# The differences of the blocks of w_co: built and split ahead, kept in DRAM, loaded as parts

## The chip, the core and the metric

The kernel runs on one core of a Trainium2 chip. Its time is the device time of one launch in microseconds (us). The core has five engines that run their own instruction streams in order and wait for one another through semaphores: TensorE (PE, matrix products), VectorE (DVE), ScalarE (ACT), GpSimd (POOL) and SyncE (SP), which here does nothing but issue DMA transfers, one after the other.

## The reference, cut to what matters

One layer of an encoder over 1024 tokens of width 1024 in float32: a mixer (window attention beside a gated delta rule), cross attention from the tokens into 256 memory tokens, and a SwiGLU feed-forward network (FFN). Each part is wrapped in RMS norms and added to the residual. The change lies in the second part:

```python
h2 = rms_norm(x1, g_cross_pre)
q = h2 @ w_cq
...
p = softmax(q_h @ k_h.T / 16)
o = concat(p @ v_h)
x2 = x1 + rms_norm(o @ w_co, g_cross_post)
```

## The kernel before, in words

**Precision.** TensorE multiplies in a reduced float32 format (F32R). Each operand is therefore split into a high and a low part by `split` (L100): ACT casts the high part (L103), DVE, or POOL where that is asked for, subtracts it from the source for the low part (L104). A product is three matmuls: high x high, high x low, low x high (`three`). One matmul of 128 x 128 by 128 x 512 is the unit. `load_w` (L119) issues one transfer of 512 KB into a `wraw` tile (L126) and splits it into `whi` and `wlo`; there are two buffers of each. Blocks under `tc.high_priority(AHEAD)` are moved up by the scheduler at build time; apart from that it lays out each engine's order from the program's order and its own estimate.

**Cross attention.** Tokens are worked in two halves of 512, hf 0 and 1. `cross_q(hf)` (L1136) makes the queries in eight products, one for each 128 columns of w_cq: load, split (the low part on POOL), 24 matmuls into `pcq`, eviction and split into `q`. `cross_attention(q, hf)` (L1145) goes over four heads: scores `pcs`, maximum and scaling on DVE (L1159, L1160), exponential on ACT (L1164), reciprocal and normalisation on DVE (L1166, L1167), transposes `pct`, their split into `cph` and `cpl`, and the product with the values `pco` (L1183). The scheduler weaves the second half's query products into the first half's attention. For the second half the evictions also make differences with the first half's result, kept in `oraw` (L1193 to L1202).

**The product with w_co.** `o @ w_co` is done in the seven-product way on 2 x 2 blocks: four blocks of `o` (two token halves by two halves of the width) and four blocks of w_co, b11, b12, b21, b22, each 512 x 512. Seven block products of 48 matmuls replace eight, in exchange for sums and differences of blocks. Two products use w_co as it is: (0, 0) and (1, 0), loaded by `load_w`. Then come, in order: Y with `s3_` by the difference in b12; Y further with `a22` by that in b21; X with `part` by that in b22; X further, tile by tile (`by_tile`), with `s1_` by that in b11, for token rows 4 to 7; X further with `s4_` by w_co's fourth block, for token rows 0 to 3. The four raw blocks are loaded into the two `wco` tiles in eight transfers of 512 KB (L1218) that stand behind the second half's query weights on SP. Differences are made in place by `minus` on DVE (L1275): those of b11 and b12 inside the first product (`sums`), those of b22 and b21 inside the second (`later`). `weight_part` (L1237) splits each 128-row slice of a difference just ahead of its use into two `wpart` buffers of a ring of nine, 16 splits in all.

**Row ends.** As the tiles of the last two products come, `second_rows` and `first_half_rows` finish the token rows: evictions (L1314), squares on ACT (L1279), gains (L1317), then `finish`: the scale (POOL's power, L1287), the residual (L1288), its store, the next norm's squares on ACT (L1291), and the normalised row (L1295 on ACT or L1297 on DVE). Residual rows come by transfers into `xr` tiles or into the `wco` tiles, which are free by then (L1351).

**What follows.** The normalised rows are transposed (`ptn`, L1394), split with the gain (L106, L107) into `x1h`, `x1l` (rows 4 to 7) and into the parts and sums T1 to T4, X22 (rows 0 to 3, L1412 to L1426). Rows 4 to 7 feed the first half of the first FFN products, and all rows the rest (`EARLY`, L1439 to L1462); their gate and up weights are two `load_w` each. After these the FFN goes on by pairs (`pair_weights`, L1478), which the change does not touch.

## Time and profile before

| | us |
|---|---|
| three runs | 1539.69, 1540.47, 1540.54 (median 1540.47) |
| the profiled execution | 1545.09 |
| its span, from the first instruction to the last | 1543.4 |
| cross attention of both halves and products with w_co | about 649 to 873 |
| row ends, transposes and first FFN products | about 867 to 955 |

A line of a view by stretches gives the stretch and its length, then for each engine its busy time in us and in brackets its instructions, then PE's granted clock as a share of full speed, the DMA engines' busy share, and what they moved in GB/s. A group's line gives source line, engine, operation, output<-inputs, shapes and count, then busy us and mean ns, then idle time before and what ended it. A line of waits gives the waiting engine and line, what it waited for, total us, times and the longest. The chain of waits is followed back from the last instruction; each piece has its start, its length and what ran or what was waited for. PE's busy time counts pipelined matmuls, so overlapping ones are not added twice.

### The profile page before, as it was taken

Reading aid. Unit: us, or ns where it says so; the run is one execution under the profiler, and the core shown is the slowest. Engines: PE = TensorE matmul, PEld = TensorE weight load, DVE = VectorE, ACT = ScalarE, POOL = GpSimd, SP = SyncE. Lnnn points to the kernel's source line nnn. Section 1 sums busy time; section 2 is a strip of 40 time slices with the busy share of each in tenths; the row PEclk is TensorE's granted clock in tenths of the full one; section 3 lists DMA queues with packets and bytes.
Section 4 is the critical chain, followed back from the end, with each engine's and each line's share of the span. In section 5 each row is a group of like instructions: output and inputs, shape, how many; then the busy total and the mean of one; then the engine's idle time right before and its main releaser. Section 6 shows DMA issues by size and latency. Waiting matters only on the chain.

```text
span 1543.4 us, 21078 instructions
## 1 busy us (share of the span) xinstructions
PE 1479.7 (96%) x7403; PEld 1240.7 (80%) x7403; DVE 1111.7 (72%) x1794; ACT 743.2 (48%) x1516; POOL 405.1 (26%) x404
## 2 busy tenths in 40 slices
PE   6999999998999899999999888999999999999997
PEld 5888888877889778888887667888888888888786
DVE  6868999786789865536388986776867554696665
ACT  5678821457557664555345664323223332454532
POOL 2020221311336203242100822343443332000021
PEclk9999999999999999999999899999999999999999
DMA  6235575857987674441332434333533333863354
GB/s 204 77 106 149 145 194 151 218 158 200 311 284 223 205 270 156 152 129 56 94 125 96 165 127 139 123 118 121 167 123 100 109 103 103 315 212 98 105 176 165
DMA packets 264167, 241.91 MB, mean 157 GB/s; under 512 B 33769, under 2 KB 203646, under 8 KB 264062
## 3 DMA queue, kind: packets, MB, share of 16 engines
q1 hardware_dynamic: 264061, 240.57, 49.8%
q8 instruction: 58, 0.95, 0.3%
q14 instruction: 48, 0.39, 0.1%
HBM read 171.02 MB, written 66.88 MB: 154 GB/s over the span
## 4 chain that ended last, share of the span: by engine, by line
PE 63%; DVE 10%; DMA 8%; ACT 4%; issue 3%; POOL 2%; SPq 2%; DVEq 0%; POOLq 0%; ACTq 0%
PE pD L1439 8%; PE pE L1439 8%; PE pA L1439 7%; PE pcq L261 6%; PE pdX L1630 6%; PE pmg L1068 5%; PE pdA L1630 4%; PE pB L1439 4%; PE psc L809 3%; PE pst L1254 2%; PE pdD L1630 2%; PE pg L261 1%; PE pco L1183 1%; PE pdX L1727 1%; PE pcs L1157 1%
## 5 line engine op out<-in xcount | busy, mean ns | idle before, releaser
L103 ACT CAST whi<-wraw 128x1024 fp32r<-128x1024 f32 x96 | 100.8, 1051 | 161.1 <-issue 38.2
L104 POOL TENSOR_TENSOR wlo<-wraw,whi 128x1024 fp32r<-128x1024 f32 x38 | 92.9, 2446 | 186.9 <-ACT whi L103 183.9
L261 PE MATMUL pg<-hlo,whi 128*128 128x512 f32 x352 | 139.7, 397 | 0.0
L261 PE MATMUL pg<-hhi,whi 128*128 128x512 f32 x352 | 139.1, 396 | 0.0
L261 PE MATMUL pg<-hhi,wlo 128*128 128x512 f32 x352 | 138.6, 394 | 0.0
L1439 PE MATMUL pA<-b,whi 128*128 128x512 f32 x352 | 113.3, 401 | 1.8 <-ACT m L1456 1.6
L104 DVE TENSOR_TENSOR wlo<-wraw,whi 128x1024 fp32r<-128x1024 f32 x58 | 74.8, 1291 | 44.2 <-ACT whi L103 41.6
L1439 PEld LDWEIGHTS pA<-b,whi 128*128 128x128 f32 x352 | 67.0, 193 | 16.8 <-ACT m L1456 2.7
L1630 PE MATMUL pdX<-dhl,whi 128*128 128x512 f32 x264 | 76.1, 390 | 1.5 <-DVE zv L1689 0.7
L261 PEld LDWEIGHTS pg<-hhi,whi 128*128 128x128 f32 x352 | 66.6, 189 | 13.5 <-ACT hhi L103 0.2
L261 PEld LDWEIGHTS pg<-hhi,wlo 128*128 128x128 f32 x352 | 66.5, 189 | 12.9
L261 PEld LDWEIGHTS pg<-hlo,whi 128*128 128x128 f32 x352 | 66.5, 189 | 12.8
L1517 POOL TENSOR_TENSOR act<-act,up 128x512 f32<-128x512 f32 x33 | 49.8, 1509 | 93.7 <-DVE up L1516 61.8
L1439 PE MATMUL pA<-b,wlo 128*128 128x512 f32 x176 | 69.8, 398 | 1.3 <-DVE wlo L104 1.3
L103 ACT CAST whi<-araw 128x1024 fp32r<-128x1024 f32 (+1 forms) x36 | 35.3, 982 | 68.0 <-PE pdX L1630 27.6
L104 DVE TENSOR_TENSOR wlo<-araw,whi 128x1024 fp32r<-128x1024 f32 (+1 forms) x36 | 40.8, 1133 | 36.0 <-ACT whi L103 35.9
L1489 POOL TENSOR_TENSOR sr<-wraw 128x512 f32<-128x512 f32 x22 | 30.0, 1365 | 130.8 <-DMA wraw<-in_w_gate_up_dram 129.7
L1664 POOL TENSOR_SCALAR frs<-sq 128x1 f32<-128x1 f32 x8 | 12.0, 1498 | 194.3 <-ACT jk L1649 193.4
L286 DVE SCALAR_TENSOR_TENSOR acc<-cp,cols,acc 128x1024 f32<-128x1024 f32 x48 | 62.1, 1296 | 0.1
L1630 PEld LDWEIGHTS pdX<-dhl,whi 128*128 128x128 f32 x264 | 49.3, 188 | 12.7 <-issue 1.1
L1439 PE MATMUL pB<-s,s1h 128*128 128x512 f32 x176 | 54.4, 390 | 3.2 <-ACT s1h L103 3.2
L1490 DVE TENSOR_TENSOR sr<-sr,wraw 128x512 f32<-128x512 f32 x22 | 36.7, 1666 | 26.7 <-POOL sr L1489 26.7
(478 smaller groups left out, 4292.1 us busy)
## 6 DMA issues: line engine op xcount, KB each, us to landing
wraw<-in_w_gate_up_dram SPq DMA_DIRECT2D x52, 512.0 KB, 3.9
kv<-d_kv SPq DMA_DIRECT2D x32, 512.0 KB, 7.2
wraw<-in_w_in_dram SPq DMA_DIRECT2D x22, 512.0 KB, 4.8
b<-in_w_down_dram SPq DMA_DIRECT2D x20, 512.0 KB, 7.7
araw<-d_as SPq DMA_DIRECT2D x20, 512.0 KB, 3.7
pz<-d_pz SPq DMA_DIRECT2D x32, 256.0 KB, 6.9
wraw<-in_w_ckv_dram SPq DMA_DIRECT2D x16, 512.0 KB, 5.7
wraw<-in_w_out_dram SPq DMA_DIRECT2D x16, 512.0 KB, 3.7
```

What stands on the lines that cost most here:

```text
L103: nc.scalar.copy(hi, src)
L104: (eng or nc.vector).tensor_tensor(lo, src, f32(hi), ALU.subtract)
L261: nc.tensor.matmul(p_, w[:, k, :], ah[a][:, k, :], start=(k == 0 and i == 0), stop=(k == nk - 1 and i == 2))
L286: nc.vector.scalar_tensor_tensor(acc, cp[:, t:t + S], taps[t], acc, ALU.mult, ALU.add)
L809: nc.tensor.matmul(out[:, d, h, :], lt[:, d, h, :], rt[:, d, h, :], start=True, stop=True)
L1068: nc.tensor.matmul(pp[t], act[a][:, k, tt], w_[:, kk, :], start=(k == 0 and i == 0), stop=(k == KT - 1 and i == 2))
L1254: nc.tensor.matmul(bank, a[:, tt], w, start=(start and i == 0), stop=(stop and i == 2), skip_group_check=not check)
L1439: nc.tensor.matmul(out_, w[a][:, k, :], xx[b_][:, k, :], start=(start and k == 0 and i == 0), stop=(k == HK - 1 and i == 2), skip_group_ch ...
L1489: nc.gpsimd.tensor_tensor(s[0], b_[:, 0:HK], b_[:, HK:], ALU.add)
L1490: nc.vector.tensor_tensor(s[1], s[0], a_[:, 0:HK], ALU.subtract)
L1517: nc.gpsimd.tensor_tensor(o_, o_, up, ALU.mult)
L1630: nc.tensor.matmul(banks[t], a[:, k - k0, tt], w, start=(first and k == 0 and i == 0), stop=(k == NB - 1 and i == 2), skip_group_check=not ...
```

## The change

The differences are no longer made from resident blocks inside the products. Ahead of the second half's query products the program now states, for each of four 128-row slices k: four loads of 256 KB (the slices of the four raw blocks) into `wpart` buffers, four differences on DVE, four splits, and eight stores of 256 KB of the parts into eight DRAM tiles `d_t` (`sum_out`). The scheduler weaves this into the query products and the first half's attention. When the products come, the parts are loaded: those of the third difference (b12) and second (b22) slice by slice into the ring (`from_ring`, eight transfers of 256 KB each), those of the fourth (b21) and first (b11) whole into tiles of opA (`resident`, four transfers of 512 KB each). The `wco` tiles and the 8 transfers of 512 KB into them are gone, as are `weight_part`, `minus`, `sums` and `later`.

With the space that becomes free: `y7` gets a tile of its own; the difference of the two halves' attention (`s3raw`) is kept in float32, so that the second half's eviction takes one DVE subtraction instead of two; the residual rows 0 to 5 go into tiles of opA (`two_rows`), rows 6 and 7 into `xr`; the first gate and up weights of the FFN are loaded and split by `load_w` at the start of Y (`first_gate`) instead of in the EARLY loop. Instructions of PE, ACT and POOL are the same in number; DVE has four fewer, and SP has 787 transfers to issue instead of 723.

```diff
--- before.py
+++ after.py
@@ -1022,6 +1022,8 @@
     def operand(pool_, tag):
         if tag == "s1":
             return [Halves(opB, b0), Halves(opB3, "b3")]
+        if tag == "s0":
+            return [Halves(opA, f"s0{c}") for c in "hl"]
         if tag in places:
             return [p_.tile([P, KT, HALF], F32R, tag=t, name=t) for p_, t in places[tag]]
         return [pool_.tile([P, KT, HALF], F32R, tag=f"{tag}{i}", name=f"{tag}{i}") for i in range(2)]
@@ -1189,19 +1191,23 @@
                     continue
                 k = ct % HK
                 if ct < HK:
-                    d_ = tx.tile([P, HALF], F32, tag="cs", name="cs")
+                    d_ = s3_raw()[:, k]
                     nc.vector.tensor_tensor(d_, raw[:, k], po, ALU.subtract)
                     split(q[0][:, k], q[1][:, k], d_)
                     continue
                 split(q[0][:, ct, :], q[1][:, ct, :], po)
                 d_ = tx.tile([P, HALF], F32, tag="cs", name="cs")
-                nc.vector.tensor_tensor(d_, po, f32(q[0][:, k]), ALU.subtract)
-                nc.vector.tensor_tensor(d_, d_, f32(q[1][:, k]), ALU.subtract)
+                nc.vector.tensor_tensor(d_, po, s3_raw()[:, k], ALU.subtract)
                 split(*(t[:, k] for t in s2_part()), d_)
                 nc.vector.tensor_tensor(raw[:, k], raw[:, k], d_, ALU.add)
                 nc.vector.tensor_tensor(raw[:, ct], raw[:, ct], d_, ALU.subtract)
 
-    part = []
+    part, kept = [], []
+
+    def s3_raw():
+        if not kept:
+            kept.append(opA.tile([P, HK, HALF], F32, tag="s0h1", name="s3raw"))
+        return kept[0]
 
     def s2_part():
         if not part:
@@ -1210,13 +1216,30 @@
 
     q0 = cross_q(0)
     cross_attention(q0, 0)
+    d_t = {n: [dram.tile([P, HK, HALF], F32, name=f"d_t{n}{c}") for c in "hl"] for n in (1, 2, 3, 4)}
+
+    def wpart(dt):
+        return rg.tile([P, HALF], dt, tag="wpart", name="wpart", bufs=9)
+
+    def sum_out(n, k, src):
+        parts = [wpart(F32R) for _ in range(2)]
+        split(*parts, src)
+        for d_, t in zip(d_t[n], parts):
+            nc.sync.dma_start(d_[:, k], f32(t))
+
+    for k in range(HK):
+        r12, r11, r22, r21 = (wpart(F32) for _ in range(4))
+        for t, i, j in ((r12, 0, 1), (r11, 0, 0), (r22, 1, 1), (r21, 1, 0)):
+            nc.sync.dma_start(t, w_co[(HK * i + k) * P:(HK * i + k + 1) * P, j * HALF:(j + 1) * HALF])
+        nc.vector.tensor_tensor(r11, r12, r11, ALU.subtract)
+        nc.vector.tensor_tensor(r12, r22, r12, ALU.subtract)
+        sum_out(3, k, r12)
+        sum_out(1, k, r11)
+        nc.vector.tensor_tensor(r22, r22, r11, ALU.subtract)
+        nc.vector.tensor_tensor(r21, r21, r22, ALU.subtract)
+        sum_out(2, k, r22)
+        sum_out(4, k, r21)
     q1 = cross_q(1)
-    wco = [opA.tile([P, KT, HALF], F32, tag=f"s0{i}", name="wco") for i in range(2)]
-    (b11, b12), (b21, b22) = ((t[:, 0:HK], t[:, HK:KT]) for t in wco)
-    for b_, i, j in ((b12, 0, 1), (b11, 0, 0), (b22, 1, 1), (b21, 1, 0)):
-        for k0 in (0, 2):
-            nc.sync.dma_start(b_[:, k0:k0 + 2], w_co[(HK * i + k0) * P:(HK * i + k0 + 2) * P, j * HALF:(j + 1) * HALF]
-                              .rearrange("(k p) n -> p k n", p=P))
     cross_attention(q1, 1)
     L2.close()
     Lk.close()
@@ -1234,11 +1257,20 @@
     def blocks(t):
         return t[:, 0:HK], t[:, HK:KT]
 
-    def weight_part(b_, k):
-        with tc.high_priority(AHEAD):
-            dh, dl = (rg.tile([P, HALF], F32R, tag="wpart", name="wpart", bufs=9) for _ in range(2))
-            split(dh, dl, b_[:, k])
-        return dh, dl
+    def from_ring(n):
+        parts = []
+        for k in range(HK):
+            parts.append([wpart(F32R) for _ in range(2)])
+            for t, d_ in zip(parts[k], d_t[n]):
+                nc.sync.dma_start(f32(t), d_[:, k])
+        return parts
+
+    def resident(n, tags):
+        hl = [opA.tile([P, HK, HALF], F32R, tag=t_, name="tw") for t_ in tags]
+        for k0 in (0, 2):
+            for t, d_ in zip(hl, d_t[n]):
+                nc.sync.dma_start(f32(t[:, k0:k0 + 2]), d_[:, k0:k0 + 2])
+        return [[t[:, k] for t in hl] for k in range(HK)]
 
     def act_part(a, k0):
         if isinstance(a, tuple):
@@ -1253,7 +1285,7 @@
         for i, (a, w) in enumerate(((ah, dh), (ah, dl), (al, dh))):
             nc.tensor.matmul(bank, a[:, tt], w, start=(start and i == 0), stop=(stop and i == 2), skip_group_check=not check)
 
-    def block_product(banks, a, b_, first=True, last=True, extra=None):
+    def block_product(banks, a, b_, first=True, last=True):
 
         for k in range(HK):
             if k % 2 == 0:
@@ -1264,15 +1296,10 @@
                     wh, wl = load_w(w_co[rows:rows + 2 * P, c0:c0 + HALF], 2, HALF)
                 dh, dl = wh[:, k % 2], wl[:, k % 2]
             else:
-                dh, dl = weight_part(b_, k)
+                dh, dl = b_[k]
             for t in range(4):
                 three(banks[t], ah[:, k % 2], al[:, k % 2], dh, dl, slice(t * P, (t + 1) * P), first and k == 0,
                       last and k == HK - 1, first and last)
-            if extra:
-                extra(k)
-
-    def minus(o_, a, b_):
-        nc.vector.tensor_tensor(o_, a, b_, ALU.subtract)
 
     def square_of(src, ch, r):
         jk = tz.tile([P, HALF], F32, tag="junk", name="junk")
@@ -1302,14 +1329,6 @@
     def four(spec):
         return [p_.tile([P, HALF], F32, tag=t_, name="pst") for p_, t_ in spec]
 
-    def sums(k):
-        minus(b11[:, k], b12[:, k], b11[:, k])
-        minus(b12[:, k], b22[:, k], b12[:, k])
-
-    def later(k):
-        minus(b22[:, k], b22[:, k], b11[:, k])
-        minus(b21[:, k], b21[:, k], b22[:, k])
-
     def add(o_, a, b_):
         nc.vector.tensor_tensor(o_, a, b_, ALU.add)
 
@@ -1318,26 +1337,27 @@
 
     LO, HI = slice(0, HALF), slice(HALF, D)
     A = four([PG] * 4)
-    block_product(A, a11, (0, 0), last=False, extra=sums)
+    block_product(A, a11, (0, 0), last=False)
     e_ = opB.tile([P, HK, HALF], F32, tag=b0 + "0", name="p1")
     for t in range(4):
         nc.scalar.copy(e_[:, t], A[t])
-    block_product(A, a12, (1, 0), first=False, extra=later)
+    block_product(A, a12, (1, 0), first=False)
     c11 = opB3.tile([P, HK, HALF], F32, tag="b30", name="c11")
     for t in range(4):
         nc.scalar.copy(c11[:, t], A[t])
+    first_gate = [load_w(w_gate_up[:, c0:c0 + P], KT, P) for c0 in (0, FF)]
     Y = four([PG] * 4)
-    block_product(Y, s3_, b12, last=False)
-    y7 = b12
+    block_product(Y, s3_, from_ring(3), last=False)
+    y7 = opA.tile([P, HK, HALF], F32, tag="s0h0", name="y7")
     for t in range(4):
         add(y7[:, t], e_[:, t], Y[t])
-    block_product(Y, a22, b21, first=False)
+    block_product(Y, a22, resident(4, ("s0l0", "s0l1")), first=False)
     for t in range(4):
         square_of(c11[:, t], 0, t)
         gained(zz[:, t, LO], c11[:, t], LO)
         add(zv[:, t], e_[:, t], Y[t])
     X = four([PN] * 2 + [PX] * 2)
-    block_product(X, tuple(part), b22, last=False)
+    block_product(X, tuple(part), from_ring(2), last=False)
     for t in range(4):
         add(zv[:, t], zv[:, t], X[t])
         square_of(zv[:, t], 0, 4 + t)
@@ -1352,8 +1372,15 @@
         res[r] = place.rearrange("p h n -> p (h n)")
 
     res = {}
-    for r, place in ((4, b21[:, 0:2]), (5, b21[:, 2:4]), (6, b22[:, 0:2]), (7, b22[:, 2:4])):
-        residual_row(r, place)
+
+    def two_rows(r, tag):
+        t = opA.tile([P, HK, HALF], F32, tag=tag, name="xr2")
+        for i in range(2):
+            residual_row(r + i, t[:, 2 * i:2 * i + 2])
+
+    two_rows(4, "s0l1")
+    residual_row(6)
+    residual_row(7)
 
     def by_tile(a, w, last, then):
         for t in range(4):
@@ -1374,9 +1401,9 @@
         add(zz[:, t, HI], e_[:, t], X[t])
         row_end(zz[:, t], t)
 
-    by_tile([act_part(s1_, k) for k in (0, 2)], [weight_part(b11, k) for k in range(HK)], False, second_rows)
-    for r, place in ((0, None), (1, None), (2, b11[:, 0:2]), (3, b11[:, 2:4])):
-        residual_row(r, place)
+    by_tile([act_part(s1_, k) for k in (0, 2)], resident(1, ("s0h1", "s0l0")), False, second_rows)
+    two_rows(0, "s0h1")
+    two_rows(2, "s0h0")
     with tc.high_priority(AHEAD):
         for k in (0, 2):
             wr = wp.tile([P, 2, HALF], F32, tag="wraw", name="wraw")
@@ -1448,7 +1475,7 @@
         sg = te.tile([P, 512], F32, tag="sg", name="sg0")
         w, A = [], []
         for i, c0 in enumerate((f * P, FF + f * P)):
-            whi, wlo = load_w(w_gate_up[:, c0:c0 + P], KT, P)
+            whi, wlo = first_gate[i] if e == 0 else load_w(w_gate_up[:, c0:c0 + P], KT, P)
             w.append(((whi[:, 0:HK], wlo[:, 0:HK]), (whi[:, HK:], wlo[:, HK:])))
             A.append(pg.tile([P, 512], F32, tag="pg", name="pA0"))
             product(A[i], w[i][0], X11)
```

## Prediction, made before the changed kernel ran

> **What bounds the kernel now.** I read the page's first part first, then a table of busy time by stretch, then what the TensorE (PE) waits for, then single instructions.
>
> ```profile
> span 1543.4 us, 21078 instructions
> PE 1479.7 (96%) x7403; PEld 1240.7 (80%) x7403; DVE 1111.7 (72%) x1794; ACT 743.2 (48%) x1516; POOL 405.1 (26%) x404
> ...
> 690.00:745.00 55.00, 55.00 (x294) 47.20 (x293) 28.34 (x49) 25.70 (x60) 15.07 (x7) 1.00 0.23 68
> 745.00:776.00 31.00, 31.00 (x153) 25.99 (x152) 11.97 (x20) 11.81 (x24) 4.20 (x2) 1.00 0.41 136
> 776.00:857.00 81.00, 77.81 (x387) 64.34 (x387) 71.13 (x117) 45.53 (x94) 9.23 (x4) 1.00 0.30 104
> 857.00:873.00 16.00, 16.00 (x72) 13.25 (x71) 13.72 (x20) 8.17 (x17) 13.54 (x13) 1.00 0.51 166
> 873.00:897.00 24.00, 15.48 (x64) 10.85 (x62) 19.68 (x26) 16.77 (x31) 21.26 (x24) 0.79 0.33 131
> 897.00:960.00 63.00, 57.42 (x251) 45.46 (x252) 47.40 (x65) 34.46 (x55) 9.24 (x7) 0.97 0.47 144
> ```
>
> After the stretch and its length stand PE, weight loads, VectorE (DVE), ScalarE (ACT) and GpSimd (POOL) in busy us, then PE's granted clock, the DMA share and GB/s. PE is the bound nearly everywhere: 96% of the span. From 690 to 776 (the second half's query products and both halves' cross attention) it is never idle, while DVE works about half of the time. From 776 to 857, where DVE makes the weight differences and their splits, DVE is at 71.13 of 81 and PE loses 3.2 us. Between the last w_co product and the first FFN products (873 to 897) PE stands for 8.5 us of 24 and its clock falls. So the change can win only in 776 to 908, and can lose only in 690 to 776 or through late data.
>
> ```profile
> PE pB L1439 <- ACT s1h L103: 3.2, 2, 2.0
> PE ptn L1394 <- DVE b L107: 2.5, 2, 2.0
> ...
> PE ptn L1394 <- DVE zl L1297: 1.6, 1, 1.6
> PE pco L1183 <- DVE cpl L104: 1.5, 2, 0.9
> ...
> PE pst L1254 <- DVE zl L1314: 1.2, 1, 1.2
> ...
> PE pst L1254 <- DVE wlo L104: 0.5, 1, 0.5
> ```
>
> These are PE's waits from 690 to 960 (total us, times, longest). The pco and pst rows, 1.5 + 1.2 + 0.5 = 3.2 us, are the whole idle time of the third stretch.
>
> **What the change takes out of 776 to 873.**
>
> ```profile
> L104 DVE TENSOR_TENSOR wpart<-wco,wpart 128x512 fp32r<-128x512 f32 x16 | 11.4, 715 | 1.4 <-PE pst L1254 1.4
> L1275 DVE TENSOR_TENSOR wco<-wco 128x512 f32<-128x512 f32 x16 | 10.3, 685 | 3.2 <-DMA wco<-in_w_co_dram 3.2
> ...
> L1199 DVE TENSOR_TENSOR cs<-cs,b 128x512 f32<-128x512 f32 x4 | 2.6, 684 | 0.0
> ...
> L103 ACT CAST wpart<-wco x16: 602/621/650, 778.3 to 848.7; 128x512 fp32r<-128x512 f32 x16
> ```
>
> 16 differences (10.3 us) and 16 low parts (11.4) leave DVE, 16 casts of 0.62 (9.9 us) leave ACT; four more DVE subtractions (2.6) are gone for good, since the difference of the two score halves is kept raw. DVE goes from 71.1 + 13.7 = 84.8 to 84.8 - 24.3 = 60.5 us of 97. The differences now come ready from DRAM, so the attention's cpl, the eviction zl and wlo no longer queue behind them. I take all 3.2 us of PE's waits as gone; the bounds are 0 (they only change their releaser) and 3.2.
>
> **The tail.** What DVE still owed at the last product's end sets the idle time after it.
>
> ```profile
> 856.41 4.66 DMA wraw<-in_w_gate_up_dram
> ...
> 867.27 1.21 DVE wco L1288
> ...
> 946.28 4.59 DMA wraw<-in_w_gate_up_dram
> ...
> 862.37 11.05 PE L1254 MATMUL pst<-part,b 128*128 128x512 f32 x48
> ...
> 883.19 1.12 PE L1394 MATMUL ptn<-ident,zl 128*128 128x128 f32 x4 [2.02 <-DVE b L107]
> ...
> 892.53 0.33 PE L1394 MATMUL ptn<-ident,zz 128*128 128x128 f32 x1 [0.66 <-DVE zz L1297]
> ...
> 893.85 0.44 PE L1394 MATMUL ptn<-ident,zz 128*128 128x128 f32 x2 [0.52 <-DVE b L107]
> 896.03 0.44 PE L1394 MATMUL ptn<-ident,zz 128*128 128x128 f32 x2 [1.74 <-ACT zz L1295]
> 897.08 0.74 PE L1439 MATMUL pA<-b,whi 128*128 128x512 f32 x2 [0.61 <-ACT m L1456]
> ...
> 907.15 0.50 PE L1439 MATMUL pA<-b,wlo 128*128 128x512 f32 x1 [1.26 <-DVE wlo L104]
> ```
>
> The first three lines are of the chain of waits, the others of PE's instructions, with the idle time before one in brackets. The first row end (L1288, row 4) starts at 867.27. Its tile was finished after the first 12 of 48 matmuls of the by-tile product before 862.37; at 11.05 / 48 = 0.23 us each that is 862.37 - 36 x 0.23 = 854.1. It came 13 us late, because ACT and DVE had stood for the FFN's gate weights (4.66 us) and DVE had a backlog. In the new order those weights are asked for at the start of Y, two products earlier, and DVE's backlog is shorter; with an eviction, a gain and a square of about 0.65 us each, partly overlapped, and POOL's power row 4 can end near 860, some 7.5 us earlier, and rows 4 to 7 are normalised near the product's end. The first pair of FFN products needs all four of those rows, eight transposed tiles and their evictions, so PE resumes at the product's end + 8.8, by my count of DVE's new order, where it was 883.19 - (862.37 + 11.05) = 9.8: 1.0 us won (bounds 0 and 3). Rows 0 to 3, which hold up the second part, do not wait behind rows 4 to 7 any more; I put them ready at + 18 instead of + 25. The idle times there, 0.66 + 0.52 + 1.74 + 0.61 + 1.26 = 4.8 us, are taken as gone (bounds 0 and 4.8).
>
> ```profile
> 876.00:880.00 4.00, 2.89 (x13) 2.25 (x13) 3.93 (x7) 3.28 (x7) 2.71 (x5) 0.65 0.02 8
> 880.00:884.00 4.00, 1.98 (x7) 1.26 (x7) 4.00 (x8) 3.71 (x7) 3.20 (x4) 0.50 0.65 262
> 884.00:888.00 4.00, 4.00 (x15) 3.23 (x14) 4.00 (x4) 2.88 (x4) 3.84 (x5) 0.57 0.17 67
> ...
> 896.00:900.00 4.00, 3.36 (x10) 2.56 (x11) 2.42 (x2) 1.52 (x3) 2.71 (x4) 0.71 0.36 132
> 900.00:904.00 4.00, 4.00 (x17) 3.14 (x17) 1.91 (x3) 1.78 (x3) 0.34 (x1) 0.87 0.01 4
> ```
>
> After each group of idle times PE works at a lower granted clock. The first drop (2.89 x 0.35 + 1.98 x 0.5 + 4.00 x 0.43 = 3.7 us) stays, as most of its idle time stays. The second (3.36 x 0.29 + 4.00 x 0.13 = 1.5 us) goes with the 4.8.
>
> **What it adds to 690 to 776.** The same 32 DVE operations and 16 casts, four rounds of: four loads of 256 KB, four differences, four splits, eight stores of 256 KB. In the built order the rounds lie between DVE positions 825 and 898, the first ahead of the first score maximum (its scaling ran at 693.78, below), the last some 70 operations on: about 690 to 745. DVE goes there from 28.34 to 28.34 + 21.7 = 50.0 us of 55; ACT from 25.7 to 35.6. PE is fully busy there, so nothing can be won; the question is what DVE's lag costs.
>
> ```profile
> 693.78 2.08 DVE L1160 TENSOR_SCALAR cmx<-cmx 128x2 f32<-128x2 f32 x1
> ...
> 693.43 2.40 POOL L104 TENSOR_TENSOR wlo<-wraw,whi 128x1024 fp32r<-128x1024 f32 x1 [4.19 <-ACT whi L103]
> ```
>
> A DVE operation on two columns takes 2.08 us, and ends with POOL's subtraction (695.83). There are seven of these in the stretch, 15.07 us of POOL. If each holds a DVE operation that reads and writes SBUF only (all 32 new ones do) for half its time, that is 7 x 1.2 = 8.4 us, of which the 28.34 already hold some 3: DVE then has about 55 of 55, and lags the attention by up to some 6 us toward the end. PE's order was built with more products left for after the attention (194 matmuls of w_co after its last tile, 160 before: 34 x 0.23 = 7.8 us), so fewer products lie between the attention's steps to cover the lag; against that, from 745 to 776 DVE has 19 us free to catch up. Bounds: 0 and 8 us (the lag uncovered, and 2 more in the first round). I take 3, nearer the low end, as PE shows no wait at all there with DVE half idle, and query products still stand between the attention's steps.
>
> The Trainium skill ("SBUF — State Buffer", section "SBUF: two separate sides") calls the port pair of DVE and GpSimd an exclusive lock held for a whole instruction, which also stops a DVE operation with two SBUF inputs. The two rows agree for the short operation, and by the rule any of the new ones can be held up to 2.4 us; that is the second rival below, priced there from rows.
>
> ```profile
> wraw<-in_w_cq_dram SPq DMA_DIRECT2D x16, 512.0 KB, 4.3
> d_a<-act SPq DMA_DIRECT2D x29, 256.0 KB, 2.8
> ...
> wco<-in_w_co_dram SPq DMA_DIRECT2D x8, 512.0 KB, 7.1
> ...
> 740.47 0.37 SPq L126 DMA_DIRECT2D wraw<-in_w_cq_dram  x1
> ...
> 751.74 1.05 ACT L103 CAST whi<-wraw 128x1024 fp32r<-128x1024 f32 x1 [3.75 <-issue]
> ```
>
> Transfers: 8 loads of 512 KB (4 MB) become 16 + 24 loads and 32 stores (20 MB), 64 more issues on the one in-order queue of SP. At 0.37 us each that is 24 us of issuing, in a stretch where the queue mostly waits; 12 MB of it in some 55 us, on top of 68 GB/s, is below 300 GB/s. The eight query weights are interleaved with the rounds on SP. The last was issued at 740.47, is landed 4.3 later, and is used at 751.74: 7 us of slack. A round takes a load (4.3, as the larger w_cq load), eight DVE operations (8 x 0.69 = 5.5), the first cast (0.6) and a store (2.8), 13.2 us, some 15 behind the attention's operations, so four end about 750: the last query weight is a few us late inside its slack, cost 0. The reloads are asked for one product or more ahead (a product of 48 matmuls lasts 11 us, a load 2.8 to 7.1): cost 0, bounds 0 and 3, for the parts of the fifth product, whose tiles come free last.
>
> **Sum.** 3.2 + 1.0 + 4.8 + 1.5 = 10.5 won, 3 lost: 7.5 us. The profiled execution took 1545.1 us (span 1543.4 and 1.7 around it), 4.6 above the median of 1540.5, so it gives 1545.1 - 7.5 = 1537.6, and taken off the median 1533.0. With the lag at 0 to 5.5 and the tail's second part half won to wholly won the forecast's own range is 1529 to 1537.4. What this kernel's measurement can tell from no change is 0.2%, 3.1 us: 1537.4 to 1543.6 is the same.
>
> **Rivals.**
> (1) The tail is not won. For: the second part's evictions and T parts follow on a DVE that is 75% busy from 897 to 960, and a wait of 3.2 us for s1h stands at the end of that stretch, behind 4.59 us for gate weights, so time won at 892 can be lost there. Against: those weights are asked for as soon as a buffer is free, so earlier too. Then 3.2 + 1.0 - 3 = 1.2 us: 1539.3.
> (2) DVE saturates: held by POOL, each of the seven subtractions costs it 2 us, 14 in all, and PE's stalls reach their bound of 8. For: the stretched operation above. Against: 31 us of half-idle DVE follow. 10.5 - 8 = 2.5 us: 1538.0 (1535 to 1541).
> (3) Slower: the rounds run through a ring of nine buffers with twelve uses a round, so the next round's loads wait on SP for DVE and for stores to land, and the query weights wait behind them; PE then stands for its weight. The price is four times what a round takes over 15 us, less the 7 us of slack and the 3 by which the last issue may slip. A round of 20 gives 20 - 10 = 10 us and cancels the gain; one of 21.5 gives 26 - 10 = 16, and 1540.5 - 10.5 + 16 = 1546. For: every operation of a round queues behind in-order attention work on DVE and ACT, and a cast that waits for a buffer stops ACT's softmax behind it. Against: DMA at a share of 0.23, and the stores' 2.8 us.
>
> **How the numbers follow.** Forecast 0.48; the same with no lag at all (1527 to 1529) 0.06; rival (1) 0.06; rival (2) 0.12, a third of it still under 1537.4; rival (3) 0.28 over 1543.6 to 1555, as its chain is the longest and least covered by rows. Faster 0.48 + 0.06 + 0.04 = 0.58, same 0.06 + 0.08 = 0.14, slower 0.28. The range 1527 to 1549 leaves out about 0.12, the longer part of rival (3).
>
> **What would show it.** Right: PE 55 of 55 or at least 52 in the stretch of the rounds with DVE above 45; no pst or pco wait over 1 us in the products; the first L1288 within 7 us of its tile; ACT's 4.66 us wait for gate weights gone; one group of idle times after the last product, not two, the clock below 1 only once. Wrong: PE waiting for cpr, cpl or a query cast in the rounds (rival 2), for whi of a query weight, with SP's loads late (rival 3), for a reloaded part; or the second group of idle times standing further on (rival 1).

## The result, and the profile after

The changed kernel ran 14 times beside 14 runs of the kernel before: median 1534.12 us (1530.37 to 1545.67) against 1542.90 (1537.62 to 1549.76); ratio 0.9947, 95% interval 0.9928 to 0.9967. A later set of 11 runs beside 33 gave 0.9968 (0.9957 to 0.9980). By these ratios it is faster by some 5 to 8 us.

These are the first part of the page after, and the same stretches as in the prediction:

```profile
span 1536.2 us, 21190 instructions
PE 1477.0 (96%) x7403; PEld 1241.1 (81%) x7403; DVE 1109.5 (72%) x1790; ACT 742.3 (48%) x1516; POOL 396.3 (26%) x404
...
690.00:745.00 55.00, 52.33 (x276) 43.40 (x275) 44.72 (x79) 32.24 (x74) 14.07 (x6) 1.00 0.78 258
745.00:776.00 31.00, 31.00 (x152) 26.00 (x151) 12.61 (x21) 13.43 (x26) 5.34 (x3) 1.00 0.72 246
776.00:857.00 81.00, 81.00 (x407) 68.68 (x406) 56.76 (x87) 39.02 (x83) 12.60 (x9) 1.00 0.36 121
857.00:873.00 16.00, 14.88 (x69) 11.99 (x67) 13.38 (x23) 10.29 (x20) 9.49 (x14) 1.00 0.80 294
873.00:897.00 24.00, 19.42 (x84) 15.39 (x85) 15.76 (x21) 16.90 (x27) 17.37 (x18) 0.79 0.24 93
897.00:960.00 63.00, 56.18 (x250) 44.99 (x250) 47.84 (x68) 32.01 (x52) 10.85 (x7) 0.97 0.44 137
```

The products from 776 to 857 run without a gap (77.81 of 81 before); DVE is at 56.76 there instead of 71.13. The price stands in the first stretch: 55 - 52.33 = 2.67 us of idle PE where there was none, with the DMA share up from 0.23 to 0.78. Behind the products (857 to 897) PE stands 5.7 us of 40, 8.5 before; but the last stretch lost more than before, 6.8 us instead of 5.6. PE's last product and its instructions that waited after it show where:

```profile
859.74 11.04 PE L1286 MATMUL pst<-part,b 128*128 128x512 f32 x48
...
872.50 0.44 PE L1421 MATMUL ptn<-ident,zl 128*128 128x128 f32 x2 [1.06 <-DVE zl L1324]
...
874.89 0.66 PE L1421 MATMUL ptn<-ident,zl 128*128 128x128 f32 x4 [1.14 <-DVE zz L1333]
878.10 1.22 PE L1466 MATMUL pA<-b,whi 128*128 128x512 f32 x2 [2.56 <-ACT b L106]
880.11 1.12 PE L1421 MATMUL ptn<-ident,zl 128*128 128x128 f32 x4 [0.79 <-DVE b L107]
932.41 0.73 PE L1466 MATMUL pA<-b,whi 128*128 128x512 f32 x2 [3.35 <-ACT m L1483]
938.76 0.73 PE L1466 MATMUL pB<-s0h,s1h 128*128 128x512 f32 x2 [2.03 <-ACT s1h L103]
```

From 880 to 929 nothing waits: the second group of idle times (892 to 907 before) is gone. A new one of 3.35 us stands at 932, at the last of the first FFN products.

To compare kernels without what happens ahead of the change, I count from the first query matmul. The rows of the tiles give it (after the colon min, median and max ns of one, then first and last start); here for after:

```profile
L261 PE MATMUL pcq<-b,whi x128: 386/390/481, 646.8 to 695.6; 128*128 128x512 f32 x128
...
L1286 PE MATMUL pst<-part,b x48: 388/389/393, 859.7 to 870.4; 128*128 128x512 f32 x48
...
L1466 PE MATMUL pB<-s0h,s1h x176: 388/390/500, 938.8 to 1294.1; 128*128 128x512 f32 x176
```

The products end 870.4 - 646.8 = 223.6 us after it (start of the last matmul), the first matmul of the pairs (the pair stage) follows 938.8 - 870.4 = 68.4 later (the tail), and the execution ends at 1536.2 - 646.8 = 889.4. The table has the same for all profiles, and the ratios of the runs.

| kernel | first query matmul at | products end | tail | end | ratio to before (95%) |
|---|---|---|---|---|---|
| before | 648.8 | 224.2 | 72.6 | 894.6 | |
| before again | 643.6 | 223.9 | 74.1 | 896.7 | 1.0012 (0.9998 to 1.0026) |
| after | 646.8 | 223.6 | 68.4 | 889.4 | 0.9947 (0.9928 to 0.9967) |
| after again | 644.7 | 223.7 | 67.8 | 889.7 | 0.9968 (0.9957 to 0.9980) |
| raw slices ahead | 647.7 | 223.4 | 66.1 | 887.2 | 0.9963 (0.9947 to 0.9979) |
| gate weights late | 645.9 | 224.0 | 65.6 | 887.8 | 0.9945 (0.9930 to 0.9959) |
| before, gate weights early | 646.7 | 226.1 | 65.7 | 889.9 | 0.9959 (0.9942 to 0.9975) |
| 24 operations back (place held) | 643.1 | 243.6 | 73.9 | 916.3 | 1.0104 (1.0081 to 1.0126) |
| 24 operations back | 644.7 | 231.8 | 68.3 | 898.3 | 1.0005 (0.9992 to 1.0017) |
| low parts on POOL | 645.6 | 224.3 | 68.7 | 890.6 | 0.9966 (0.9951 to 0.9980) |
| before, gate early, POOL | 643.6 | 227.5 | 66.0 | 891.4 | 0.9957 (0.9941 to 0.9974) |
| ahead and POOL | 645.1 | 221.7 | 69.3 | 888.5 | 0.9967 (0.9954 to 0.9980) |
| ahead, gate late | 642.4 | 219.5 | 68.6 | 886.7 | 0.9955 (0.9939 to 0.9971) |
| differences on POOL | 645.7 | 227.6 | 65.3 | 891.6 | 0.9981 (0.9970 to 0.9991) |

The change's own worth in the traces is 6.1 us: (894.6 + 896.7) / 2 against (889.4 + 889.7) / 2. Of that 0.4 lies in the products and 5.3 in the tail; the rest lies behind the tail. The tail's gain is only in part idle time: PE stands 12.9 and 11.9 us in the tails before, 11.1 and 10.3 after, 1.8 less, while its busy time for the same 258 instructions falls from 59.6 and 62.1 to 57.2 and 57.4, 3.5 less. Another 2.0 us of the difference of the first two spans lies ahead of the first query matmul, which came between 642.4 and 648.8 in 14 profiles: that is spread, and no part of the change. The runs cannot tell kernels apart that differ by 2 or 3 us. The traces from a common point come closer, but two profiles of one kernel still differ there by 2.1 us (before) and 0.3 us (after) at the end.

### The profile page after: what moved, and what is told of

The parts are those of the page before. It is cut to its first block, busy times and chain, and to the rows that moved or that the text cites. A ratio compares the mean times of both kernels' runs of the same rounds, so it can differ in the third digit from the quotient of the medians.

```text
span 1536.2 us, 21190 instructions
## 1 busy us (share of the span) xinstructions
PE 1477.0 (96%) x7403; PEld 1241.1 (81%) x7403; DVE 1109.5 (72%) x1790; ACT 742.3 (48%) x1516; POOL 396.3 (26%) x404
## 4 chain that ended last, share of the span: by engine, by line
PE 70%; DVE 11%; DMA 8%; ACT 6%; issue 3%; SPq 1%; POOL 1%; DVEq 0%; POOLq 0%; ACTq 0%
PE pE L1466 8%; PE pD L1466 8%; PE pA L1466 7%; PE pg L261 6%; PE pmg L1070 6%; PE pdX L1657 6%; PE pcq L261 4%; PE pdA L1657 4%; PE pB L1466 4%; PE pst L1286 3%; PE psc L809 2%; PE pdX L1754 2%; PE pdD L1657 2%; DVE acc L286 2%; DMA wraw<-in_w_ckv_dram 1%
## 5 line engine op out<-in xcount | busy, mean ns | idle before, releaser
L261 PEld LDWEIGHTS pg<-hhi,whi 128*128 128x128 f32 x352 | 66.5, 189 | 13.3 <-ACT hhi L103 0.2
L261 PEld LDWEIGHTS pg<-hhi,wlo 128*128 128x128 f32 x352 | 66.5, 189 | 12.8
L261 PEld LDWEIGHTS pg<-hlo,whi 128*128 128x128 f32 x352 | 66.4, 189 | 12.7
L286 DVE SCALAR_TENSOR_TENSOR acc<-cp,cols,acc 128x1024 f32<-128x1024 f32 x48 | 62.1, 1295 | 0.1
L1691 POOL TENSOR_SCALAR frs<-sq 128x1 f32<-128x1 f32 x8 | 11.9, 1496 | 193.6 <-ACT jk L1676 192.7
L1466 PE MATMUL pB<-s0h,s1h 128*128 128x512 f32 x176 | 54.4, 391 | 3.4 <-ACT s1h L103 3.4
L103 ACT CAST dhl<-b 128x512 fp32r<-128x512 f32 x66 | 40.3, 620 | 31.6 <-PE pdA L1657 13.7
```

The source lines that it names most:

```text
L103: nc.scalar.copy(hi, src)
L261: nc.tensor.matmul(p_, w[:, k, :], ah[a][:, k, :], start=(k == 0 and i == 0), stop=(k == nk - 1 and i == 2))
L286: nc.vector.scalar_tensor_tensor(acc, cp[:, t:t + S], taps[t], acc, ALU.mult, ALU.add)
L1466: nc.tensor.matmul(out_, w[a][:, k, :], xx[b_][:, k, :], start=(start and k == 0 and i == 0), stop=(k == HK - 1 and i == 2), skip_group_ch ...
```

## The experiments

**The loss in the rounds.** What ended DVE's waits in the rounds (680 to 745 of after), and pieces of its chain of waits:

```profile
DVE wpart L1234 <- DMA wpart<-in_w_co_dram: 8.9, 4, 3.9
...
DVE wpart L1235 <- DMA wpart<-in_w_co_dram: 1.2, 1, 1.2
...
712.86 5.12 DMA wpart<-in_w_co_dram
718.00 0.70 DVE wpart L1234
```

DVE isn't full there (44.72 of 55). It stands, in order, at the first difference of a round until that round's raw slice has landed, and the attention's maximum, scaling and evictions behind it stand too. SP's queue shows when the raw loads of each round go out:

```profile
685.08 1.95 SPq L1233 DMA_DIRECT2D wpart<-in_w_co_dram  x4
...
698.85 2.90 SPq L1233 DMA_DIRECT2D wpart<-in_w_co_dram  x4
...
712.21 2.26 SPq L1233 DMA_DIRECT2D wpart<-in_w_co_dram  x4
...
727.62 0.38 SPq L1233 DMA_DIRECT2D wpart<-in_w_co_dram  x1
```

They go when the ring has places again, in rounds of 13.8, 13.4 and 15.4 us. To test that this is what costs, the raw slices of three rounds went to a place that is empty until the attention writes it:

```diff
+    def raw_loads(k):
+        ts = [raw[:, HK * (k > 0) + i] for i in range(4)] if k < 3 else [wpart(F32) for _ in range(4)]
...
+    ahead = [raw_loads(0), raw_loads(1)]
     for k in range(HK):
-        r12, r11, r22, r21 = (wpart(F32) for _ in range(4))
+        r12, r11, r22, r21 = ahead[k]
...
+        if 0 < k < 3:
+            ahead.append(raw_loads(k + 1))
+    cross_attention(q0, 0)
```

> The raw slices of the first three rounds land in the still empty tile of the attention's result (oraw) instead of the ring, two rounds at once and ahead of the attention; only the fourth uses the ring. Theory: in the rounds DVE stands in order behind a difference whose raw load is late (7.5 + 1.2 us of waits on it in the profile of after), and this makes PE's 2.7 us of stalls there. Then DVE's waits for raw loads fall under 3 us, PE's stalls between 690 and 745 under 1 us, and the time from the first query matmul to the end of the last w_co matmul falls from 224.0 to 222 or 222.5; about 1.5 us faster than the changed kernel. Rival (DVE is full, held by POOL): the same DVE work is there, so PE's stalls stay at 2 to 3 us and 224.0 stays.

DVE's waits for raw loads fell from 10.1 (8.9 + 1.2) to 3.5 us (2.2 + 1.3). PE's three stalls became one of 2.12, and behind that one stands the fourth round, the only one that still uses the ring:

```profile
719.41 2.03 DVE L1238 TENSOR_TENSOR wpart<-wpart 128x512 f32<-128x512 f32 x1 [2.15 <-DMA wpart<-in_w_co_dram]
721.37 0.68 DVE L104 TENSOR_TENSOR b<-pco,b 128x512 fp32r<-128x512 f32 x1
...
722.10 0.85 PE L1175 MATMUL pct<-ident,cpr 128*128 128x128 f32 x4 [2.12 <-DVE b L104]
```

The difference L1238 waits 2.15 us for its load, takes 2.03 instead of 0.69 (a subtraction of POOL runs from 718.53 to 720.89), and PE waits for the eviction behind it. So the rows show the mechanism at the one stall that is left, but the numbers that were to follow did not come: DVE's waits 3.5 us (under 3 expected), PE's stalls 2.12 (under 1; the rival said 2 to 3), the end of the products 223.4 (222 to 222.5), where a lowered clock took back some 1.4 us. With the gate weights late as well, the order that the build laid out had no such stall:

```diff
     (raw slices ahead, and)
-    first_gate = [load_w(w_gate_up[:, c0:c0 + P], KT, P) for c0 in (0, FF)]
...
-            whi, wlo = first_gate[i] if e == 0 else load_w(w_gate_up[:, c0:c0 + P], KT, P)
+            whi, wlo = load_w(w_gate_up[:, c0:c0 + P], KT, P)
```

> The raw slices ahead together with the gate weights asked for late again: the two single edits had 289.5 and 289.6 us from the first query matmul to the first pair matmul, the changed kernel 292.0. Theory (each took a different loss of the changed kernel away): 287 to 288.5, and some 3 us faster than the changed kernel. Rival (both figures are the changed kernel's own spread): 289 to 292.

```profile
690.00:745.00 55.00, 55.00 (x297) 47.26 (x296) 38.49 (x69) 31.63 (x73) 14.55 (x6) 1.00 0.80 263
```

PE is busy all through the rounds, the products end at 219.5, 4.1 us earlier than in after, with the same DMA traffic (share 0.80) and the same DVE work. So neither the traffic nor the amount of DVE work costs by itself. Of the 4.1 us 2.7 are the stalls; the other 1.4 are PE's busy time for the same 1105 instructions, 219.6 us instead of 221.0, and no run shows why. DVE's and PE's order in the rounds also differs a little from that of the run with the raw slices ahead alone, so the last stall's end is not the loads' alone. But the tail is 68.6 again, so the end comes 2.9 us earlier in the trace, and the runs (0.9955) cannot tell it from the changed kernel. The 288.1 us to the first pair matmul are the theory's (287 to 288.5), the 3 us in the runs can't be seen. Then the rival of a full DVE held by POOL was put to the test by giving POOL the differences:

```diff
-        nc.vector.tensor_tensor(r11, r12, r11, ALU.subtract)
+        nc.gpsimd.tensor_tensor(r11, r12, r11, ALU.subtract)
     (and the other three)
```

> The changed kernel with the 16 differences made by POOL, so that a difference that stands for its raw load no longer stands in DVE's order. Theory (the loss in the rounds is DVE standing in order for raw loads): DVE's waits for them, 8.7 us, vanish, and PE's 2.7 us of stalls between 690 and 745 fall to 1.5 or less, less what POOL's slower subtractions cost. Rival (POOL's subtractions hold DVE's operations that read SBUF only): POOL's busy time grows by some 20 us, DVE's operations stretch, and PE's stalls grow to 4 to 8.

The stretch of the rounds and DVE's groups in it, with the differences on POOL, and then two of the same groups in after:

```profile
690.00:745.00 55.00, 50.38 (x260) 42.79 (x259) 43.18 (x60) 29.57 (x70) 29.03 (x17) 0.94 0.64 210
...
L104 DVE TENSOR_TENSOR wpart<-wpart 128x512 fp32r<-128x512 f32 x12 | 15.0, 1268 | 5.5 <-ACT wpart L103 5.5
L1169 DVE TENSOR_TENSOR cpr<-cpr,csum 128x512 f32<-128x512 f32 x8 | 10.6, 1323 | 0.3
L1161 DVE TENSOR_REDUCE cmx<-pcs 128x2 f32<-128x512 f32 x8 | 5.5, 682 | 3.8 <-PE pcs L1159 3.8
...
L104 DVE TENSOR_TENSOR cpl<-pct,cph 128x512 fp32r<-128x512 f32 x6 | 4.1, 683 | 0.3 <-ACT cph L103 0.2
```

```profile
L104 DVE TENSOR_TENSOR wpart<-wpart 128x512 fp32r<-128x512 f32 x16 | 12.5, 793 | 0.0
L1169 DVE TENSOR_TENSOR cpr<-cpr,csum 128x512 f32<-128x512 f32 x8 | 5.5, 687 | 0.2
L1161 DVE TENSOR_REDUCE cmx<-pcs 128x2 f32<-128x512 f32 x8 | 5.5, 683 | 0.0
```

The rival's number came: 55 - 50.38 = 4.6 us of stalls, more at a lowered clock. With POOL busy for 29 us DVE's low parts take 1268 ns instead of 793 and the normalisation 1323 instead of 687, while what reads PSUM, where PE's results lie (cmx 682, cpl 683), doesn't change. But the run doesn't separate the two causes, since the late load still holds DVE. POOL now stands for it, ACT's cast of the difference behind POOL, and DVE in order at the low part behind the cast. These are two pieces of the chain of waits, and DVE's low part:

```profile
703.00 6.96 DMA wpart<-in_w_co_dram
710.12 1.30 POOL wpart L1235
```

```profile
712.10 1.23 DVE L104 TENSOR_TENSOR wpart<-wpart 128x512 fp32r<-128x512 f32 x1 [4.83 <-ACT wpart L103]
```

So both are real, and POOL is the worse place for the work. In after, with 14 us of POOL there, the 16 low parts are stretched by 16 x (793 - 687) = 1.7 us together, against 10.1 us of waits for raw loads; that the load is the larger cause there is read from these rows. The run with raw slices ahead and gate weights late fits: it has as much POOL work (14.55 us), hardly a wait for a raw load (1.0 us) and no stall.

**The tail: the relief of DVE or the early gate weights?** One part at a time:

```diff
     (the changed kernel)
-    first_gate = [load_w(w_gate_up[:, c0:c0 + P], KT, P) for c0 in (0, FF)]
...
     (the kernel before)
+    first_gate = [load_w(w_gate_up[:, c0:c0 + P], KT, P) for c0 in (0, FF)]
     Y = four([PG] * 4)
```

> The changed kernel with the first gate and up weights asked for in the loop of the first FFN products again. Measured from the first query matmul to the first matmul of the pair stage: before 296.8 us, after 292.0. Theory (both the early weights and the DVE relief make the tail's gain): ACT's wait of some 4 us for the weights comes back ahead of the row ends, and the distance is 293.5 to 296; products still end at 224. Rival G (the early weights alone make the gain): 296.8. Rival N (the relief of DVE alone): 292.0.

> The kernel before with one part of the change: the first gate and up weights asked for at the start of Y. Theory: ACT's 4.66 us wait is gone but DVE's backlog stays, 294 to 296 us from the first query matmul to the first pair matmul (before 296.8), products end at 224.6 as before. Rival G: 292.0, the change's whole gain. Rival N: 296.8.

Each part alone makes a tail of 65.6 or 65.7 us, 7 to 8 less than before, and both together 68. From the first query matmul to the first pair matmul it is 289.6 us with the relief of DVE alone and 291.8 with the early weights alone, 292.0 with both and 296.8 before. The theory (they add) doesn't hold, and of the rivals G (the early weights alone) meets its number in the second run only and N (the relief alone) comes near its own, 292.0, in the first only: each part alone is enough. Both bring the row ends forward, the first of them from 6.2 us ahead of the products' end to 12.7 (relief alone) and 11.4 (early weights alone), 14.8 with both. Without the early request, ACT's wait for gate weights is small all the same, as the first line (with late gate weights) shows against the second (before):

```profile
ACT whi L103 <- DMA wraw<-in_w_gate_up_dram: 1.6, 2, 1.1
```

```profile
ACT whi L103 <- DMA wraw<-in_w_gate_up_dram: 4.9, 2, 4.6
```

With the relieved DVE the low parts that free the `wraw` buffers come sooner, so the loads are asked for from 845 on instead of at 850 and 856. What the early request alone doesn't give are the products: they ended at 226.1, with 2.8 us of a wait of pst for the eviction zl and a lowered clock. The kernel before with that one part (0.9959) can't be told from the whole change by its runs.

To see whether the amount of DVE work counts in the products, 24 operations were put back. The first way held the tile of the kept difference:

```diff
+            for _ in range(more):
+                nc.vector.tensor_tensor(s3_raw()[:, k], s3_raw()[:, k], s3_raw()[:, k], ALU.max)
...
-    block_product(A, a11, (0, 0), last=False)
+    block_product(A, a11, (0, 0), last=False, more=2)
```

> The changed kernel with 24 more DVE operations of 128x512 in place on the kept difference (a maximum with itself, which changes nothing) in the first three products, 16.5 us of the 24.3 that the change took out of there. Theory (DVE's amount of work made the waits in the products and the late row ends): PE waits 1 to 3 us in the products again, which end at 225 to 227 after the first query matmul instead of 224.0, and the tail loses up to 2 more. Rival (the waits came from the raw blocks' late landing and the order, not from the amount): 224.0 and 292.0 stay.

```profile
862.93 13.30 PE L1286 MATMUL pst<-tw,b 128*128 128x512 f32 x48 [16.50 <-DMA tw<-d_t1h]
```

This run says nothing of the amount: the reload of the first difference, which goes into that tile, was issued at 858.9 instead of 829.2, right behind the last of the 24 operations (which started at 858.2), and PE stood 16.5 us for it. It shows what a reload costs in this scheme when it waits for its place. The second way writes rows that nothing reads (`za[:, k]` from `raw[:, k]`):

> The changed kernel with 24 more DVE operations of 128x512 in its first four products, into rows that are written anew later, so that no load and no tile waits for them: 16.5 us of the 24.3 that the change took out. Theory (DVE's amount of work in the products makes the waits there and the late row ends): PE waits 1 to 3 us in the products, which end 225 to 227 us after the first query matmul instead of 223.6, and the tail, from there to the first pair matmul, stays near 68.4, since the early gate weights hold it. Rival (order and landing, not the amount): 223.6 stays.

```profile
840.00:864.00 24.00, 19.52 (x77) 15.67 (x76) 24.00 (x27) 6.67 (x14) 13.47 (x8) 0.86 0.36 121
...
852.75 13.23 PE L1286 MATMUL pst<-tw,b 128*128 128x512 f32 x48 [4.48 <-issue]
```

All 24 started between 826.5 and 862.9, since the source is complete only then, and not spread over the products as the differences had been. There DVE is full (24.00 of 24, 16.60 in after) and PE loses 4.48 us at once and more by its clock (48 matmuls in 13.23 us instead of 11.04). The profile names nothing for this wait; DVE's first `zl<-zl,pst`, which reads the banks that the product writes, ran at 851.98, just ahead of its end. The products end 8.2 us later than in after, the tail stays at 68.3, and the whole gain is gone (1.0005). The sign is the theory's, the size is three times as large, and as the work stood so close together, the run doesn't say what the same amount costs when it is spread.

**The new wait at 932.** Its chain of waits in after, below the piece of the first row end (L1315, used further down):

```profile
855.97 1.28 DVE xr L1315
...
923.47 1.14 DVE wlo L104
924.60 0.56 DVE s0l L104
925.16 6.07 DMA wraw<-in_w_gate_up_dram
931.38 0.40 issue
931.78 0.59 ACT m L1483
```

The low part that frees the buffer stands behind the parts of T in DVE, the next load goes out only at 925.16, and ACT's queue holds the copy m behind the cast of what it brings. So the low parts went to POOL:

```diff
-            whi, wlo = first_gate[i] if e == 0 else load_w(w_gate_up[:, c0:c0 + P], KT, P)
+            whi, wlo = first_gate[i] if e == 0 else load_w(w_gate_up[:, c0:c0 + P], KT, P, nc.gpsimd)
```

> The changed kernel with the low parts of the second to fourth pair of gate and up weights made by POOL, which does nothing from 900 to 930, instead of by DVE. Theory: in the changed kernel the tail's second group of idle times is gone, but part comes back at 932 (PE waits 3.35 us for ACT's copy m), because the low part that frees the buffer for the next gate load stands in DVE behind the parts of T; on POOL it does not, so that wait falls under 1 us, and the distance from the end of the last w_co matmul to the first pair matmul falls from 68.4 to 65.5 or 66.5. Rival: PE arrives earlier at the pair stage and waits there for s1h as much longer: 68.4 stays.

> The changed kernel with the raw slices ahead (as in the run with raw slices ahead) and the low parts of the later gate weights on POOL. Theory: products end near 223.4, tail 64 to 65 instead of 66.1, so 2 to 4 us faster than the changed kernel, and the fastest of all. Rival: the tail's cap is the pair stage's wait for s1h, and it stays at 66.

> The kernel before with the first gate and up weights asked for at the start of Y, and the low parts of the next three pairs on POOL; nothing of the round trip through DRAM. With the early weights alone the products ended at 226.1 and the tail took 65.7 us. Theory: its tail had only 0.7 + 0.6 us of such waits, so 64.5 to 66: as fast as the whole change or 1 us faster. Rival: POOL's subtractions of 2.4 us hold DVE's parts of T, and the tail grows by 1 to 3.

The wait shrank only to 1.60, four small ones (0.53, 0.41, 0.76 and 0.88) came with it, and the tails are 68.7, 69.3 and 66.0: nothing won in any of the three (65.5 to 66.5, 64 to 65 and 64.5 to 66 were expected; without POOL it is 68.4, 66.1 and 65.7). DVE's groups from 890 to 935 say why, first in after, then with POOL:

```profile
L104 DVE TENSOR_TENSOR b<-r,b 128x512 fp32r<-128x512 f32 x8 | 5.4, 686 | 0.0
L1446 DVE SCALAR_TENSOR_TENSOR r<-ptn,cols,r 128x512 f32<-128x512 f32 x4 | 3.0, 748 | 2.7 <-PE ptn L1421 2.7
...
L104 DVE TENSOR_TENSOR s0l<-oraw,s0l 128x512 fp32r<-128x512 f32 x4 | 2.7, 684 | 0.0
```

```profile
L104 DVE TENSOR_TENSOR b<-r,b 128x512 fp32r<-128x512 f32 x8 | 8.3, 1038 | 0.3 <-ACT b L103 0.3
L104 DVE TENSOR_TENSOR s0l<-oraw,s0l 128x512 fp32r<-128x512 f32 x4 | 4.7, 1163 | 0.0
...
L1446 DVE SCALAR_TENSOR_TENSOR r<-ptn,cols,r 128x512 f32<-128x512 f32 x4 | 3.0, 743 | 0.8 <-PE ptn L1421 0.8
```

DVE operations with both inputs in SBUF grow from 686 to 1038 and from 684 to 1163 ns; the one that reads PSUM stays (748 and 743). What DVE gives away it pays back in waiting.

**Spread.** Both kernels once more:

> The changed kernel again, unchanged, for a second profile. If the differences of 2 to 3 us in the tail between the changed kernel (68.4) and the runs with late gate weights (65.6) or raw slices ahead (66.1) belong to the kernels, this run shows 68 or more; if they are the spread of one program, 65 to 67. The loss in the rounds should be 2.5 to 3 us again.

> The kernel before again, unchanged, for a second profile. Theory: from the first query matmul the products end at 224.2 again and the tail takes 72 to 73 with two groups of idle times; the first query matmul itself, at 648.8 in the first profile and between 643 and 648 in eight others with the same code ahead of it, comes earlier. Rival: 648.8 again, and part of the gain lies ahead of the change.

Both repeat: after with stalls of 2.8 us in the rounds, a wait of 2.99 us for m, and a tail of 67.8; before with two groups of idle times, 223.9 and 74.1. The first query matmul came at 643.6. So one program's own spread of the tail is 0.6 us (after) to 1.5 us (before). The 65.6 of the run with late gate weights lies 2.2 and 2.8 us below after's two; the mark set for this was 68 or more, and 67.8 misses it narrowly. That the difference belongs to the kernels is likely but not certain, as that kernel has one profile.

## Why the prediction was right, step by step

- **Products, 3.2 us won: right.** No pst matmul waits in after. DVE's busy time from 776 to 873 was forecast too low, though: 70.1 us (56.76 + 13.38) and not 60.5, as row ends, among others, moved in from behind 873 (six of L1315, four of L1288 before).
- **Rounds, 3 us lost: the size was right (2.67 and 2.8), the reason wrong.** I had DVE full, 55 of 55, and held by POOL. It worked 44.72, and from 680 to 745 it stood 10.1 us in order for raw loads. As the 3 was picked between bounds of 0 and 8, that the size came out is luck. The step that failed is the one that took the lag from DVE's busy time; the round of "some 15 us" had all that was needed (13.4 to 15.4 measured), but I used it only for the query weights behind the loads on SP, which did come in time, and not for the difference ahead of the attention on DVE. Rival (3)'s mechanism was there, at a small scale; rival (2)'s shows where POOL has more to do, beside the late load.
- **Row ends: right.** The first one starts at 855.97 in after, 14.8 us ahead of the products' end (859.74 + 11.04); before it was 6.2 ahead (867.27 against 873.42). That is 8.7 earlier, predicted 7.5.
- **First group, 1.0 us won: half of it at most.** PE resumes at the products' end + 9.3 (880.11 - 870.78), predicted 8.8. Its idle time in the group is no shorter: 5.7 us (5.2 again) against about 5 in both profiles before.
- **Second group, 4.8 us won: the wrong step of the sum.** It went as said, but it did not leave one group of idle times only: 3.35 us (2.99 again) came back at 932, where before had 0.27 + 0.72. The net is 4.8 - 2.4 = 2.4. Rival (1) had looked for this at the pair stage; it stands one product earlier.
- **Clock, 1.5 us won: about so on the mean, for another reason.** Busy time x (1 - clock), summed over 2 us windows of the tail, is 5.5 and 8.2 us in the two profiles before, 5.2 and 5.3 in those after: 1.6 less on the mean, but 0.3 less than in the profile from which the 1.5 were taken. The second drop did not go, it moved along with the idle time, to 932. PE's busy time in the tail fell by more than this, by 3.5 us; what the other 1.9 are, no run shows.
- **Early gate weights: the wait went, the worth was wrong.** I had both parts working together. Each alone gives the tail, and together they give 2 to 3 us less.
- **Sum:** predicted 7.5 us and 1533.0. The runs say 1534.12, 8.8 under the median of before beside it, the second set of them 5.9 (1537.03 against 1542.92), and the traces 6.1. By the traces the sum was too high by 1.4, and its parts are not those of the forecast: of the 6.1 the idle time of PE up to the pair stage makes some 2 (3.2 + 1.0 + 4.8 - 3 = 6.0 in the sum) and its shorter busy time in the tail 3.5 (1.5 in the sum). That 1534.12 lies so near 1533.0 is luck in part: 1533.0 was reckoned from a median of 1540.5 over three runs of the kernel before, and over 14 runs that median is 1542.90.

What stays open is why late gate weights leave 2 to 3 us less tail in the changed kernel. The rows say where it lies: PE's idle time is about the same (10.6 us, 11.1 and 10.3 in after), but the same 258 instructions take 55.0 us instead of 57.2 and 57.4, at a granted clock of 0.95 instead of 0.90. Late weights don't always do this: with the raw slices ahead as well the tail is 68.6, with early ones 66.1. The orders of the builds differ in more than that line, and no run took this apart.

## What to carry to other kernels

Work that is moved from a busy stretch into one where an engine is half idle can cost what its first instruction waits for more than what it lasts: an in-order engine that stands for a load holds all behind it, so let the loads go a round ahead of the work. Giving the work to another engine did not free it here, as the engine stood for what came out of that work. Try each part of a change alone before building the rest; here the early request alone brought the first pair matmul forward as far as the whole change did, 291.8 us against 292.0, as either part brings the first row end 5 to 6.5 us forward. A stall that was removed late in a stage showed up again at the next buffer that was freed late.

## What the runs showed of the hardware

With POOL subtracting, DVE operations with two SBUF inputs took up to 1.9 times as long (687 to 1323 ns) and those that read PSUM the same (683 and 682). The Trainium skill ("SBUF — State Buffer", section "SBUF: two separate sides") has a DVE operation with two SBUF inputs and a POOL operation that reads SBUF exclude each other for a whole instruction. The trace agrees.

Two stalls of PE of one length cost differently. With raw slices ahead PE waited 2.12 us at 722, and the clock fell; with the POOL low parts beside it, it waited 2.07 us at 719 and nothing fell (1.00 from 720 to 730 too):

```profile
720.00:730.00 10.00, 7.90 (x31) 6.57 (x32) 10.00 (x18) 5.23 (x15) 0.90 (x1) 0.83 0.69 219
```

```profile
710.00:720.00 10.00, 7.93 (x50) 6.96 (x49) 7.73 (x15) 5.43 (x15) 2.36 (x1) 1.00 0.73 236
```

The first lost 7.90 x 0.17 = 1.3 us more. The Trainium skill ("TensorE: Matmul & The Clock Gate", section "What's actually happening") has the clock halved after an idle window of about 3.4 us, on windows that run free of the kernel. Here a wait of 2.12 us was enough in one of two cases; that the place in the window decides would fit, and wasn't tried.
